# Spreading group B's scale factors with 64-column products whose stationary operand is one column at step zero

## The chip, the core and the metric

The kernel runs on one core of a Trainium2 chip. The metric is the device time of one execution in microseconds (us), smaller is better. Five engines work side by side: TensorE (PE) multiplies, VectorE (DVE) and ScalarE (ACT) work elementwise, GpSimd (POOL) does small work and SyncE (SP) starts the transfers. A matmul of PE takes a *stationary* operand (`lhsT`, loaded into the array) and a moving one (`rhs`, streamed through), and writes to PSUM.

## The reference, cut to what matters

Two layers, each with three groups of attention heads (A, B, C), an output projection and a feed-forward part. The change touches group B, differential attention:

```python
def diff_block(qb1, qb2):
    p = (softmax(scores(qb1, k1_all, sb)) - lam * softmax(scores(qb2, k2_all, sb)))
    return weigh(p, vb_all)

ob = sweep_blocks(diff_block, group(q1, B_HEADS), group(q2, B_HEADS))
ob = rmsnorm(ungroup(ob), g_subln) * (1.0 - lam_init)
```

There are 512 latent tokens and 256 context tokens, four B heads of 64 columns. In the second layer the context tokens need no output.

## The kernel before, in words

Group B goes two heads and 256 query tokens at a time (`attn_b`). There are ten such pieces: six in layer 0 (two pairs of heads, each with two pieces of latent and one of context queries) and four in layer 1. A piece makes scores `S` in PSUM, exponentials `P` on ACT, subtracts the second softmax from the first on DVE (`P1 = P2 * cf + P1`), transposes `P` on PE (products `T<-ident,P`), copies the transposes out (`pt`), and multiplies them with the values `V` into `acc`, a PSUM tile `T`. In `acc` the output lies transposed: partitions 0 to 63 are the first head, 64 to 127 the second, and the 256 columns are tokens.

Then comes the RMS norm of each token and head, a chain over all engines: ACT squares `acc` (`sqb`); PE sums the squares over each head's 64 partitions with two products whose moving operand `hsel` has two columns (written `T<-hsel,sqb`); DVE makes `ms` from these sums; POOL raises it to a power (`rs`, printed `t<-t,mhalf`). `rs` holds four factors per token: token on the partitions, (token block, head) in the columns. PE *spreads* them, that is brings them to the layout of `acc` (head's 64 partitions, token in the column), by a product with the identity. ACT or DVE copies the result out (`rsb`), and DVE multiplies `acc` with it into `o`, which the output projection reads after a split in high and low parts (`oh`, `ol`).

All instructions are recorded first and then put into one order by a planner (`Plan.schedule`), which prices every operation, looks which engine is free next and takes the ready operation that is earliest in the program's order, with an advance for score products. It also charges a fixed price where PE goes from products with 128 output partitions to products with 64 or 32, or back, and takes what is recorded under `plan.together()` as one piece. The engines then run their own queue in this order. All instructions therefore carry one line, L377, in the profile, and are told apart by tiles. Output tiles of 64 partitions were in the program before: the products with `V` are made in pairs, one head to partitions 0 to 63 and the other to 64 to 127. A stationary operand at step zero was there too: `T<-brow,ident` in the norm of A's queries and keys.

Of the kernel before, what the change touches and what calls it, by code (L numbers as in the profile page):

```python
# [47 lines left out]
MODE_AHEAD = 30  # L48
SA = 0.125
SB = 32.0 ** -0.5  # L50
SLOTS = {"u": 39, "pt": 8, "s": 7, "y": 24, "rb": 2, "S": 2, "T": 4, "ropeG": 1}


class _Op:
# [17 lines left out]
class Plan:  # L72
# [171 lines left out]
    def schedule(self):  # L244
# [8 lines left out]

        level = {tag: np.zeros(n + 1, np.int32) for tag in SLOTS}
        for t, a in self.first.items():
            level[self.tile_tag[t]][a:self.last[t] + 1] += 1
        for tag, lv in level.items():
            if lv.max() > SLOTS[tag]:
                raise ValueError(f"{tag}: {lv.max()} tiles alive of {SLOTS[tag]} at {ops[int(lv.argmax())].tag}")
        slots = {tag: [0.0] * b for tag, b in SLOTS.items()}  # L260
        t_end = dict.fromkeys(to_go, 0.0)
# [19 lines left out]
        while len(order) < n:  # L281
            best = None
            for e in sorted(free_at, key=free_at.get):
# [4 lines left out]
                while heap and len(seen) < 250:  # L288
# [21 lines left out]
                    for tag, ts in need.items():  # L310
# [5 lines left out]
                        at = max(at, sorted(slots[tag])[k - 1])  # L316
                        if b > frontier and level[tag][frontier:b].max() + k > SLOTS[tag]:
                            full[tag] = b
# [62 lines left out]
def dit_block(  # L381
# [8 lines left out]
    plan = Plan(nc, (  # L390
        x, c, ctx_in, c_ctx, w_ada, b_ada, g_attn, g_ffn, w_in, g_q, g_k, lam_q1, lam_k1, lam_q2, lam_k2,
        g_subln, sink_logit, w_out, w_ff1, w_ff3, w_ff2, g_final, k_ident, k_mask, k_ones, k_ropeA, k_ropeB, out))
    act, dve, pe, pool, sp = (plan.queue(e) for e in ("act", "dve", "pe", "pool", "sp"))
    act_dve, dve_pool = plan.queue("act|dve"), plan.queue("dve|pool")

    pools = {tag: ctx.enter_context(tc.tile_pool(name="p" + tag, bufs=SLOTS[tag])) for tag in ("u", "pt", "s", "y", "rb")}
    cp = ctx.enter_context(tc.tile_pool(name="cp", bufs=1))
    pools["S"] = ctx.enter_context(tc.tile_pool(name="pS", bufs=SLOTS["S"], space=PSUM))
    pools["T"] = ctx.enter_context(tc.tile_pool(name="pT", bufs=SLOTS["T"], space=PSUM))
# [4 lines left out]
    def nm(s):  # L404
        cnt[0] += 1
        return f"{s}{cnt[0]}_"

    def new(tag, shape, name, dt=F32):
        return plan.tile(pools[tag], [128] + list(shape), dt, tag, nm(name))

    def U(shape, dt=F32, name="u"):
        return new("u", shape, name, dt)
# [4 lines left out]
    def tiny(n):  # L417
        return new("y", [n], "t")
# [7 lines left out]
    def C(shape, name, dt=F32):  # L426
        return cp.tile([128] + list(shape), dt, tag=name, name=name)
# [13 lines left out]
    ident = C([128], "ident")  # L441
# [233 lines left out]
    for l in range(2):  # L675
# [71 lines left out]
        for ch, segs in enumerate(chunks):  # L747
            o = 0
# [67 lines left out]
        ropeG = plan.tile(cp, [128, 2, NX, 2, 64], F32, "ropeG", f"ropeG{l}")  # L816
# [197 lines left out]

        def spread(rps, o, rr, n):

            rb = new("rb", [6, 64], "rb")
            dve_pool.tensor_copy(rb[:, 0:2 * n], rr.rearrange("p (h o) -> p h o", o=1).to_broadcast([128, 2 * n, 64]))
            for j in range(n):
                pe.matmul(rps[:, o + 128 * j:o + 128 * j + 128],  # L1020
                          lhsT=rb[:, 2 * j:2 * j + 2].rearrange("p h d -> p (h d)"), rhs=ident, start=True, stop=True)

        def pv_pair(acc, Ps, off, heads, kbs):

# [85 lines left out]
        def attn_b():  # L1110
            for p, r, i0 in units(range(2)):
# [31 lines left out]
                rs = tiny(4)  # L1143
                pool.tensor_tensor(rs, ms, mhalf[:, 0:4], ALU.pow)
                spread(acc, 256, rs, 2)
                rsb = S2([256], "rsb")
                act_dve.copy(rsb, acc[:, 256:512])
# [113 lines left out]
        for r, i in ctx_first:  # L1261
# [14 lines left out]
            for j, kt in enumerate(range(KT)):  # L1276
                with plan.together():
                    for n, (st, wl) in enumerate(((oh, 0), (oh, 1), (ol, 0))):
                        for hf in range(2):
                            pe.matmul(ps[hf], lhsT=st[:, kt], rhs=wo[kt][wl][:, 512 * hf:512 * hf + 512],  # L1280
                                      start=(j == 0 and n == 0), stop=(j == KT - 1 and n == 2))
# [164 lines left out]
        for ft in range(FT):  # L1446
# [18 lines left out]
            for a in range(2):  # L1465
                if ft:
                    hs.append(PS())
                s = hs[a]
# [48 lines left out]
        for n, (r, i) in enumerate(qtiles):  # L1517
            plan.label = f"ffE{l}"
            xt = xt0[r, i]
            if last:  # L1520

                y, ss = U([1024], name="yo"), tiny(2)
# [82 lines left out]
```

## Time and profile before

| | us |
|---|---|
| median of 3 runs | 1688.7 (1687.33 to 1689.38) |
| the profiled execution's own time | 1688.15 |
| its span, first to last instruction | 1686.3 |
| PE busy | 1636.0 (97%) |
| DVE busy | 1308.3 (78%) |
| ACT busy | 724.6 (43%) |
| POOL busy | 117.9 (7%) |

The span leaves 1.85 us of the execution's own time around it. The busy shares are means over stages: projections and feed-forward part, where PE is all that counts, and two stretches of attention, about 200 to 390 us (layer 0) and 1140 to 1290 us (layer 1), where the four compute engines hand work to one another. Records of a PE product are longer than the distance to the next one, since products overlap: what a product costs is read from its start to the start of the next.

### The profile page before, as it was taken

The page shows a single profiled execution, that of the slowest core. Times are in us where ns is not written, and L with a number is a line of the kernel's source. Part 1 is how long each engine was busy: PE and PEld are TensorE (multiplying, and loading weights), DVE is VectorE, ACT ScalarE, POOL GpSimd, SP SyncE. Part 2 cuts the span into 40 slices and gives each one's busy share as a digit, 9 for nine tenths or more (in the row PEclk, how much of TensorE's full clock was granted, in tenths as well). Part 3 has the DMA queues.
Part 4 walks back from the last instruction along what each step waited for, and adds up shares of the span by engine and source line. Part 5 has one row for each costly group of instructions (what it writes and reads, how often), then busy time and mean ns, then how long its engine had stood idle before and what let it go on. Part 6 is the DMA issues. An engine that isn't in the chain of part 4 may idle for free.

```text
span 1686.3 us, 24082 instructions
## 1 busy us (share of the span) xinstructions
PE 1636.0 (97%) x9171; PEld 1330.1 (79%) x9171; DVE 1308.3 (78%) x2238; ACT 724.6 (43%) x1441; POOL 117.9 (7%) x167
## 2 busy tenths in 40 slices
PE   7999899999999999999999999999999999999998
PEld 4787667667898888888888888777777888888886
DVE  3776889776576997987768884788886668888896
ACT  3523888774354222323211152368884542232222
POOL 0130300100000000000000001121001000000010
PEclk9999999999999999999999999999999999999999
DMA  9512231225353554443323360112023534234261
GB/s 307 204 51 75 62 97 38 82 69 144 96 191 102 175 160 152 141 147 124 103 76 87 138 188 25 38 48 55 1 55 109 150 100 126 75 101 124 75 200 50
DMA packets 153278, 182.94 MB, mean 108 GB/s; under 512 B 9316, under 2 KB 121396, under 8 KB 153164
## 3 DMA queue, kind: packets, MB, share of 16 engines
q1 hardware_dynamic: 153164, 181.42, 34.8%
q8 instruction: 72, 1.18, 0.3%
q14 instruction: 42, 0.34, 0.1%
HBM read 163.00 MB, written 9.47 MB: 102 GB/s over the span
## 4 chain that ended last, share of the span: by engine, by line
PE 82%; DVE 4%; ACT 4%; issue 1%; DMA 0%; POOL 0%; DVEq 0%; SPq 0%; POOLq 0%; ACTq 0%
PE S__1355 L377 1%; PE S__1354 L377 1%; PE S__1543 L377 1%; PE S__1765 L377 1%; PE S__1841 L377 1%; PE S__1468 L377 1%; PE S__1691 L377 1%; PE S__1908 L377 1%; PE S__2047 L377 0%; PE S__2045 L377 0%; PE S__2036 L377 0%; PE S__2034 L377 0%; PE S__1969 L377 0%; PE S__1378 L377 0%; PE S__1365 L377 0%
## 5 line engine op out<-in xcount | busy, mean ns | idle before, releaser
L377 POOL TENSOR_TENSOR t__2091<-t__2090,mhalf 128x1 f32<-128x1 f32 x1 | 0.5, 548 | 513.8 <-DVE t__2090 L377 513.8
L377 POOL TENSOR_TENSOR ws__3615<-ws__3615,gate__3614 128x512 f32<-128x512 f32 x1 | 1.3, 1298 | 285.9 <-DMA ws__3618<-in_w_ff_dram 285.9
L377 DVE TENSOR_TENSOR wl__2247<-ws__2245,wh__2246 128x1024 fp32r<-128x1024 f32 x1 | 1.2, 1227 | 10.9 <-ACT V__2170 L377 10.9
L377 ACT ACT_TABLE_LOAD x6 | 7.7, 1283 | 0.8 <-PEq L1590 0.7
L377 DVE SCALAR_TENSOR_TENSOR acc__1463<-wa__1465,cstat,acc__1463 128x1024 f32<-128x1024 f32 x1 | 1.3, 1285 | 8.1 <-ACT acc__1463 L377 8.1
L377 DVE TENSOR_TENSOR t__2200<-qr__2199,ropeB 128x128 f32<-128x128 f32 x1 | 0.3, 292 | 9.2 <-ACT qr__2199 L377 9.2
L377 ACT ACTIVATE xn__2088<-xf__2066 128x1024 f32<-128x1024 f32 x1 | 1.1, 1060 | 13.5 <-issue 13.5
L377 ACT CAST fh__1972<-sg__1929 128x384 fp32r<-128x384 f32 x1 | 0.5, 514 | 12.7 <-DVE sg__1929 L377 12.7
L377 DVE TENSOR_TENSOR sg__1356<-sg__1356,S__1355 128x768 f32<-128x768 f32 x1 | 1.0, 954 | 5.8 <-ACT acc__1374 L377 5.8
L377 ACT ACTIVATE sg__1895<-S__1884 128x768 f32<-128x768 f32 x1 | 0.8, 812 | 10.9 <-PE S__1884 L377 10.9
L377 ACT ACTIVATE sg__1958<-S__1947 128x768 f32<-128x768 f32 x1 | 0.8, 812 | 10.8 <-PE S__1947 L377 10.8
L377 PE MATMUL T__115<-wa__116,cstat 128*32 128x128 f32 x8 | 0.7, 417 | 4.9 <-DVE t__98 L377 4.9
L377 ACT ACTIVATE sg__2021<-S__2010 128x768 f32<-128x768 f32 x1 | 0.8, 812 | 10.6 <-PE S__2010 L377 10.6
L377 ACT ACTIVATE sg__2035<-S__2034 128x768 f32<-128x768 f32 x1 | 0.8, 812 | 10.4 <-PE S__2034 L377 10.4
L377 ACT CAST gh__2002<-sg__1990 128x768 fp32r<-128x768 f32 x1 | 0.8, 837 | 9.6 <-DVE sg__1990 L377 9.6
L377 ACT CAST wh__1728<-ws__1727 128x1024 fp32r<-128x1024 f32 x1 | 1.1, 1052 | 8.6 <-DMA ws__1727<-in_w_ff_dram 8.6
L377 ACT CAST wh__1577<-ws__1576 128x1024 fp32r<-128x1024 f32 x1 | 1.1, 1052 | 8.5 <-PE T__1568 L377 8.5
L377 ACT CAST wh__1502<-ws__1501 128x1024 fp32r<-128x1024 f32 x1 | 1.0, 1047 | 8.3 <-PE T__1493 L377 8.3
L377 POOL TENSOR_TENSOR ropeG<-ropeA,gqk 128x64 f32<-128x64 f32 (+1 forms) x7 | 4.1, 608 | 7.0 <-DVE gqk L377 5.7
L377 ACT CAST wh__1656<-ws__1655 128x1024 fp32r<-128x1024 f32 x1 | 1.1, 1052 | 8.1 <-DVE yw__1408 L377 8.1
L377 ACT ACTIVATE acc__1687<-wa__1686,cstat 128x1024 f32<-128x1024 f32 x1 | 1.1, 1150 | 7.8 <-PE T__1667 L377 7.8
L377 ACT ACTIVATE acc__1837<-wa__1836,cstat 128x1024 f32<-128x1024 f32 x1 | 1.1, 1150 | 7.8 <-PE T__1813 L377 7.8
(14049 smaller groups left out, 6742.8 us busy)
## 6 DMA issues: line engine op xcount, KB each, us to landing
x__83<-in_x_dram SPq DMA_DIRECT2D x1, 512.0 KB
x__84<-in_x_dram SPq DMA_DIRECT2D x1, 512.0 KB
x__131<-in_x_dram SPq DMA_DIRECT2D x1, 512.0 KB
x__136<-in_x_dram SPq DMA_DIRECT2D x1, 512.0 KB, 6.4
x__198<-in_ctx_dram SPq DMA_DIRECT2D x1, 512.0 KB
x__203<-in_ctx_dram SPq DMA_DIRECT2D x1, 512.0 KB
ws__240<-in_w_in_dram SPq DMA_DIRECT2D x1, 512.0 KB
ws__243<-in_w_in_dram SPq DMA_DIRECT2D x1, 512.0 KB
```

The costliest lines, as they stand in the source:

```text
L377: getattr(self.real[op.eng], method)(*args, **kw)
```

## The change

`spread` no longer makes `rb`, the tile in which each factor is repeated 64 times along the columns (ten copies of 128x256, on DVE or POOL as the planner chose). The stationary operand is the column of `rs` itself, read 64 times at step zero. For this each product of 128 output partitions is cut into two of 64, one per head, and a piece's four products go together.

```diff
-SLOTS = {"u": 39, "pt": 8, "s": 7, "y": 24, "rb": 2, "S": 2, "T": 4, "ropeG": 1}
+SLOTS = {"u": 39, "pt": 8, "s": 7, "y": 24, "S": 2, "T": 4, "ropeG": 1}
...
         def spread(rps, o, rr, n):
 
-            rb = new("rb", [6, 64], "rb")
-            dve_pool.tensor_copy(rb[:, 0:2 * n], rr.rearrange("p (h o) -> p h o", o=1).to_broadcast([128, 2 * n, 64]))
-            for j in range(n):
-                pe.matmul(rps[:, o + 128 * j:o + 128 * j + 128],
-                          lhsT=rb[:, 2 * j:2 * j + 2].rearrange("p h d -> p (h d)"), rhs=ident, start=True, stop=True)
+            with plan.together():
+                for j in range(n):
+                    for h in range(2):
+                        pe.matmul(rps[64 * h:64 * h + 64, o + 128 * j:o + 128 * j + 128],
+                                  lhsT=rr[:, 2 * j + h:2 * j + h + 1].to_broadcast([128, 64]), rhs=ident, start=True, stop=True)
```

Since the planner sees one step less between `rs` and the product, and other prices, it also orders the attention stretches anew. PE's order is the same up to the attention of layer 0, between the two attention stretches and after the second. Tile numbers are lower in the changed kernel, by 3 at the first spread and by one more with each that follows. Three places matter to the prediction.

The first spread of layer 0, on PE, at about 200 us; first before, then changed:

```order
L377 MATMUL T__433<-hsel,sqb__446 128x2 x2
L377 MATMUL T__488<-ident,stq__485 128x128 x2
L377 MATMUL T__488<-ident,stk__486 128x128 x2
L377 MATMUL S__575<-bkc__348,bqc__347 128x256 x2
L377 MATMUL T__618<-ident,stbq__619 128x128 x2
L377 MATMUL T__618<-ident,stbk__620 128x128 x2
L377 MATMUL S__579<-bkc__348,bqc__347 128x256 x2
L377 MATMUL T__433<-ident,rb__450 128x128 x2
L377 MATMUL T__621<-ident,stbq__622 128x128 x2
```

```order
L377 MATMUL T__430<-hsel,sqb__443 128x2 x2
L377 MATMUL T__484<-ident,stq__481 128x128 x2
L377 MATMUL T__484<-ident,stk__482 128x128 x2
L377 MATMUL S__570<-bkc__345,bqc__344 128x256 x2
L377 MATMUL T__612<-ident,stbq__613 128x128 x2
L377 MATMUL T__612<-ident,stbk__614 128x128 x2
L377 MATMUL T__430<-ident,t__446 64x128 x4
L377 MATMUL S__574<-bkc__345,bqc__344 128x256 x2
L377 MATMUL T__615<-ident,stbq__616 128x128 x2
```

The spread (`T<-ident,rb`, now `T<-ident,t`) has moved ahead of one pair of score products.

The third of the four pieces of layer 1, on PE, at about 1223 us. Here `S<-kc`, `S<-kx` and `S<-maskR` are group C's scores, `T<-ident,P` transposes of C's exponentials. Before:

```order
L377 MATMUL S__2801<-maskR,identR 128x384
L377 MATMUL T__2730<-hsel,sqb__2743 128x2 x2
L377 MATMUL T__2772<-ident,P__2755 128x128
L377 MATMUL T__2772<-ident,P__2761 128x128
L377 MATMUL T__2772<-ident,P__2767 128x128
L377 MATMUL S__2806<-kc__2527,qx__2524 128x256 x2
...
L377 MATMUL S__2807<-maskR,identR 128x384
L377 MATMUL T__2730<-ident,rb__2747 128x128 x2
```

Changed:

```order
L377 MATMUL S__2783<-maskR,identR 128x384
L377 MATMUL T__2719<-hsel,sqb__2732 128x2 x2
L377 MATMUL T__2719<-ident,t__2735 64x128 x4
L377 MATMUL S__2788<-kc__2516,qx__2512 128x256 x2
L377 MATMUL S__2788<-kx__2514,qx__2512 128x384
```

Twenty rows of scores and transposes stood between the sums and the spread; now the spread stands directly behind the sums on which it depends.

The end of layer 1's attention, on PE, at about 1270 us: `T<-pt,V` are the products with the values of the last piece but one, `T<-ident,P` the transposes of the last piece, `T<-wh,oh`, `T<-wl,oh`, `T<-wh,ol` the output projection. Before:

```order
L377 MATMUL T__2914<-pt__2926,V__2170 64x256 x2
L377 MATMUL T__2959<-ident,P__2929 128x128
L377 MATMUL T__2959<-ident,P__2944 128x128
L377 MATMUL T__2959<-ident,P__2935 128x128
L377 MATMUL T__2959<-ident,P__2950 128x128
```

Changed:

```order
L377 MATMUL T__2902<-pt__2914,V__2161 64x256 x2
L377 MATMUL T__3001<-wh__2967,oh__2999 128x512
L377 MATMUL T__3002<-wh__2967,oh__2999 128x512
L377 MATMUL T__3001<-wl__2968,oh__2999 128x512
L377 MATMUL T__3002<-wl__2968,oh__2999 128x512
L377 MATMUL T__3001<-wh__2967,ol__3000 128x512
L377 MATMUL T__3002<-wh__2967,ol__3000 128x512
L377 MATMUL T__2947<-ident,P__2917 128x128
L377 MATMUL T__2947<-ident,P__2932 128x128
L377 MATMUL T__2947<-ident,P__2923 128x128
L377 MATMUL T__2947<-ident,P__2938 128x128
```

Six products of the output projection have come ahead of the transposes. On DVE, at the same place, before:

```order
L377 CAST wh__2980<-ws__2979 128x1024
L377 SCALAR_TENSOR_TENSOR t__2957<-t__2927,nlam,t__2956 128x2
L377 CAST wh__2983<-ws__2982 128x1024
L377 SCALAR_TENSOR_TENSOR P__2944<-P__2945,t__2957,P__2944 128x768
L377 SCALAR_TENSOR_TENSOR P__2950<-P__2951,t__2957,P__2950 128x768
L377 TENSOR_TENSOR wl__2981<-ws__2979,wh__2980 128x1024
```

Changed:

```order
L377 CAST wh__2967<-ws__2966 128x1024
L377 SCALAR_TENSOR_TENSOR t__2945<-t__2915,nlam,t__2944 128x2
L377 TENSOR_TENSOR wl__2968<-ws__2966,wh__2967 128x1024
L377 SCALAR_TENSOR_TENSOR P__2932<-P__2933,t__2945,P__2932 128x768
L377 SCALAR_TENSOR_TENSOR P__2938<-P__2939,t__2945,P__2938 128x768
```

One cast has gone from ahead of the two subtractions, and the difference `wl` has come ahead of them.

## Rows read from the trace of the kernel before

**Rows 1.** The page: span, and busy time and instructions of each engine.

```profile
span 1686.3 us, 24082 instructions
PE 1636.0 (97%) x9171; PEld 1330.1 (79%) x9171; DVE 1308.3 (78%) x2238; ACT 724.6 (43%) x1441; POOL 117.9 (7%) x167
```

**Rows 2.** Windows over both attention stretches: length, busy per engine, PEclk, DMA, GB/s.

```profile
200.00:390.00 190.00, 177.50 (x1305) 128.18 (x1306) 158.95 (x353) 149.88 (x383) 18.66 (x30) 0.98 0.31 84
...
1140.00:1290.00 150.00, 143.03 (x983) 106.72 (x980) 128.30 (x259) 120.66 (x270) 18.85 (x27) 0.98 0.20 50
```

**Rows 3.** Waits of PE, 195 to 390 us: releaser, total, times, longest.

```profile
PE S__546 L377 <- ACT P__578 L377: 2.9, 1, 2.9
PE S__1184 L377 <- ACT P__1168 L377: 1.9, 1, 1.9
...
PE S__579 L377 <- ACT P__513 L377: 1.4, 1, 1.4
```

**Rows 4.** Windows of 10 us at the end of layer 1's attention, columns as above.

```profile
1260.00:1270.00 10.00, 10.00 (x78) 7.02 (x76) 9.43 (x15) 8.25 (x18) 2.12 (x2) 1.00 1.03 252
1270.00:1280.00 10.00, 6.23 (x34) 5.01 (x32) 10.00 (x15) 6.22 (x13) 0.80 (x1) 0.66 0.69 161
```

**Rows 5.** Timeline of PE there: start, duration, operation, [idle before and releaser].

```profile
1274.27 0.48 PE L377 MATMUL T__2959<-ident,P__2944 128*128 128x128 f32 x1 [3.53 <-DVE P__2944 L377]
...
1278.88 0.42 PE L377 MATMUL T__2969<-ident,P__2929 128*128 128x128 f32 x1
1279.09 0.42 PE L377 MATMUL T__2969<-ident,P__2944 128*128 128x128 f32 x1
```

**Rows 6.** Timeline of DVE there.

```profile
1273.21 1.01 DVE L377 SCALAR_TENSOR_TENSOR P__2944<-P__2945,t__2957,P__2944 128x768 f32<-128x768 f32 x1
...
1275.07 1.21 DVE L377 TENSOR_TENSOR wl__2981<-ws__2979,wh__2980 128x1024 fp32r<-128x1024 f32 x1
```

**Rows 7.** The tile of the first spread: its copy, minimum/median/maximum in ns.

```profile
L377 DVE COPY rb__450<-t__449 x1: 295/295/295, 200.6 to 200.6; 128x256 f32<-128x256 f32 x1
```

**Rows 8.** Timeline of PE around a step-zero operand and a spread of layer 0.

```profile
239.61 0.63 PE L377 MATMUL T__456<-brow,ident 24*32 24x256 f32 x8
240.17 0.50 PE L377 MATMUL S__741<-kx__460,qx__458 128*128 128x512 f32 x1
...
241.32 0.60 PE L377 MATMUL T__594<-ident,rb__603 128*128 128x128 f32 x4
241.76 0.27 PE L377 MATMUL T__660<-ident,P__637 128*128 128x128 f32 x1
241.87 0.27 PE L377 MATMUL T__660<-ident,P__644 128*128 128x128 f32 x1
```

**Rows 9.** Timeline of PE: from a transpose to paired products of 64 output partitions.

```profile
243.30 0.27 PE L377 MATMUL T__676<-ident,P__671 128*128 128x128 f32 x1
243.51 0.65 PE L377 MATMUL T__651<-pt__653,V__214 128*64 128x256 f32 x4
...
246.34 0.60 PE L377 MATMUL T__651<-pt__659,V__215 128*64 128x256 f32 x4
246.77 0.60 PE L377 MATMUL T__651<-pt__661,V__216 128*64 128x256 f32 x4
```

**Rows 10.** Timeline of PE from two of layer 1's sums; one spread, one projection product.

```profile
1222.84 0.50 PE L377 MATMUL T__2730<-hsel,sqb__2743 128*128 128x2 f32 x4
1223.20 0.31 PE L377 MATMUL T__2772<-ident,P__2755 128*128 128x128 f32 x1
...
1226.08 0.61 PE L377 MATMUL T__2730<-ident,rb__2747 128*128 128x128 f32 x4
...
1283.70 0.39 PE L377 MATMUL T__3015<-wh__2980,ol__3013 128*128 128x512 f32 x1
1283.93 0.50 PE L377 MATMUL T__2958<-hsel,sqb__2971 128*128 128x2 f32 x4
```

**Rows 11.** Timeline of POOL: the power behind each of these two sums.

```profile
1224.01 1.01 POOL L377 TENSOR_TENSOR t__2746<-t__2745,mhalf 128x4 f32<-128x4 f32 x1 [6.52 <-DVE t__2745 L377]
...
1284.79 2.05 POOL L377 TENSOR_TENSOR t__2974<-t__2973,mhalf 128x4 f32<-128x4 f32 x1 [12.12 <-DVE t__2973 L377]
```

More of the change, by code (lines that the diff above doesn't have):

```diff
@@ L394, in dit_block @@
     act_dve, dve_pool = plan.queue("act|dve"), plan.queue("dve|pool")
-    pools = {tag: ctx.enter_context(tc.tile_pool(name="p" + tag, bufs=SLOTS[tag])) for tag in ("u", "pt", "s", "y", "rb")}
+    pools = {tag: ctx.enter_context(tc.tile_pool(name="p" + tag, bufs=SLOTS[tag])) for tag in ("u", "pt", "s", "y")}
     cp = ctx.enter_context(tc.tile_pool(name="cp", bufs=1))
```

## The prediction, made before the changed kernel had run

> **What bounds the kernel now.** The page comes first: PE is busy 97% of the span, so the time is PE's work plus what it waits [rows 1]. The view by windows shows where it waits: 177.5 of 190 us busy in layer 0's attention and 143.0 of 150 in layer 1's, so about 12.5 and 7 us of idle time lie there, while DVE is busy 84% and 86% and ACT 79% and 80% of these stretches [rows 2]. The change acts only there. The list of PE's waits then says which engine ends them: in layer 0 mostly ACT, by an exponential `P` that scores wait for (2.9, 1.9 and 1.4 us) [rows 3]. In layer 1 one wait stands out, 3.53 us at 1274 us for DVE's `P__2944` [rows 5]; the windows show that the granted clock falls there from 1.00 to a mean of 0.66 [rows 4]. No spread is on either list as a waiting instruction of any weight. Before, PE had enough other work between the sums of squares and the spread: at 1223 us from 1223.20 to 1226.08, 2.88 us, while POOL's power ended at 1225.02 [rows 10, 11].
>
> **The products themselves.** A spread costs 0.44 us of PE today (241.32 to 241.76, four records, two for each product) [rows 8]. Afterwards it is eight records of half the columns. Products of 64 output partitions already run in pairs side by side: four records of 256 columns take 0.43 us (246.34 to 246.77), half of what one after another would take [rows 9]. I price the new spread by this row: again 0.43 us, change nothing. If they ran one after another it would be 0.43 more each, 10 x 0.43 = +4.3; that end goes to a rival. The zero step costs nothing by the nearest row: eight records of 128 columns in 32-wide pieces with `brow` take 0.56 us to the next product [rows 8], which is 0.43 of work and a switch of 0.1 (next); the bound above is that 0.13 per spread, 1.3 in all, if it were the step.
>
> **Switches.** From one transpose to the next PE needs 0.11 us (241.76 to 241.87) [rows 8]; from the last transpose to products of 64 partitions 0.21 (243.30 to 243.51) [rows 9]. So a change of output width costs 0.10. Along PE's order there are 15 more of them than before (91 to 100 in layer 0's attention, 60 to 66 in layer 1's); that is fewer than two per spread because some spreads stand next to value products. 15 x 0.10 = **+1.5** (0 if they all fall into waits). The Trainium skill (TensorEngine Tiling (Array Packing), Key Properties) speaks against this change: a change of tiling mode drains the engine. By that the price would be a product's whole record less its spacing, 0.27 - 0.11 = 0.16, hence 15 x 0.16 = 2.4 and a sum 0.9 higher; the row has 0.10, and I follow the row.
>
> **The copies.** Ten `rb` copies go, eight on DVE at 0.28 to 0.35 us (0.295 at the first) [rows 7] and two on POOL. 8 x 0.29 = 2.3 us leave an engine that is 85% busy and that ends the largest wait of layer 1 [rows 2, 5]; what is saved ahead of such a wait is saved in full, elsewhere nothing. POOL is busy a tenth, so its two count for nothing. I take **-1.0** (0 to -2.3).
>
> **Where the spreads stand now.** The step between power and product has gone, and the planner puts products close behind the sums. What must be covered is sums to the power's end less the sums' own 0.36 (1222.84 to 1223.20): 1225.02 - 1222.84 - 0.36 = 1.82 at the third piece of layer 1, and 1286.84 - 1283.93 - 0.36 = 2.55 at its fourth, where the power takes 2.05 instead of 1.01 [rows 10, 11].
> At the first spread of layer 0 the product moves into the 1.4 us wait of the scores behind it [rows 3]: **-0.4** (its own 0.44 [rows 8]; 0 if its factors come only at the wait's end).
> At the other five of layer 0, PE's work in between, counted by the order and priced by such spacings, goes from 2.9 to 4.9 us to 2.0, 2.1, 2.3, 3.1 and 3.4. With 1.82 that hides, with 2.55 the first three lack 0.55 + 0.45 + 0.25. I take **+0.3** (0 to 1.25).
> In layer 1 the cover becomes 2.2, 1.6, 0 and 1.4 us (was 2.2 to 4.1). Third piece: nothing stands between, so PE waits 1.82 and the handing over, **+1.9**, against none today; behind it wait C's scores, then ACT's exponentials. Fourth: six projection products, 6 x 0.23 (1283.70 to 1283.93) = 1.4 [rows 10], against 2.55 or, with the short power, 1.5: 0.1 to 1.2, **+0.5**. Second: 0.25 to 1.0, **+0.6**. First: 0 to 0.35, **+0.2**.
>
> **Where orders moved otherwise.** At 364 us of layer 0 scores move ahead of value products and their wait of 1.9 us [rows 3] moves to the next scores; walking through ACT's order I find gain and loss alike, 0 (-1 to +1). At the end of layer 1's attention six projection products come into the place of the 3.53 us wait [rows 5], but DVE now makes the 1.21 us `wl` ahead of the two subtractions (and one cast less) [rows 6], so these come half a microsecond later. Going through both queues with the durations of these rows, PE's waits come to 2.75 instead of 3.53 + 0.24. That is -1.0. Transposes also ran 0.21 apart there instead of 0.11 (1278.88 to 1279.09) [rows 5, 8]: the lower of the clock's two levels, 1.2 GHz, for 23 of them, 2.4 us in all, after PE had idled 3.5 us. With the idle time broken up by products I give it half a chance not to fall, -1.2. Together **-2.2** (0 to -3.8).
>
> **Sum.** +1.5 - 0.4 + 0.3 + 1.9 + 0.5 + 0.6 + 0.2 - 2.2 - 1.0 = **+1.4 us**, so the span goes from 1686.3 to 1687.7, the profiled execution from 1688.15 to 1689.55, and the median, 0.55 above that execution, from 1688.7 to **1690.1**. A measurement of this kernel can tell about 0.2%, 3.4 us, from no change, so this is none (1685.3 to 1692.1).
>
> **Rivals.**
> *The chain behind the sums stays long everywhere* (slower, 0.30). One mechanism: POOL's power takes 2.05 us, as beside DVE's `wl` at 1284.79, and not 1.01 [rows 11], so every spread needs a cover of 2.55. Layer 1 then pays 2.55 + 1.15 + 1.0 + 0.35 = 5.05 and layer 0 1.25, 6.3 in place of 3.5: sum +4.2, **1692.9**. Without the tail's -2.2 it is 1695.1. It decides from +3.4 on, which is reached when the chain is some 0.3 us longer at each of the seven tight places. For it: the covers were cut to about the chain's best case. Against: the power at 1224.01 took 1.01, and a spread that waits gives its wait back where the next product would have waited anyway. The Trainium skill (GPSIMD Engine Reference, Key points) names a cause: POOL shares its SBUF interfaces with DVE, and contends with DVE's instructions of two SBUF inputs, which `wl` is; the trace agrees at 1284.79.
> *The tail heals* (faster, 0.18). If the clock never falls at 1270 us and the copies' 2.3 us all count, the terms are +1.5 - 0.4 + 0 + 1.9 + 0.1 + 0.25 + 0 - 3.8 - 2.3 = -2.75, and -3.75 with the better end at 364 us: **1685.0**. For it: DVE ends that wait, and six products fill it. Against: the subtractions come later than before.
> *The halves run one after another* (slower, 0.06): the change then doubles what it was to leave alone, +1.4 + 4.3 = +5.7, **1694.4**. Against it stand the pairs of value products [rows 9].
>
> **How the numbers follow.** No measurable change has 0.46. Slower: 0.30 + 0.06 = 0.36. Faster: 0.18. The likeliest case by itself spans 1686.5 to 1692. The range must reach into both others: down to 1683.5 (the healing tail and 1.5 us of shorter waits in layer 0), up to 1697.0 (the long chain without the tail's gain, 1695.1, and the upper bounds at 364 us, +1, and of the switches, +0.9); one in ten may lie outside on either side.
>
> **What would show it.** PE's timeline at the new spreads: eight records within 0.45 to 0.65 us say side by side, 0.9 says the opposite. PE's waits should list `T<-ident,t` for POOL's power: 1.8 to 2.0 us at the third piece of layer 1 (some 20 rows earlier than 1226), 0.3 to 1.2 at the second and fourth, next to nothing in layer 0. POOL's powers: 1.0 or 2.0. The window 1270 to 1280 shows whether the clock keeps 1.0, and the wait for DVE's `P` whether it fell below 1 us. DVE should be busy 2.3 us less over the two stretches. I am wrong if waits that I count singly cancel: a spread that waits 1.9 us lets ACT and DVE catch up, so that PE's later waits shrink; or if the new order makes a wait at a place where PE has none today, which the trace of before cannot show.

## The result, and the profile after

The changed kernel takes 1698.74 us, the median of 4 runs (1695.89 to 1701.69), against 1689.04 for the kernel before on the same chip (1687.33 to 1690.07): a ratio of 1.006, with a 95% interval of 1.0047 to 1.0073. It is slower by 9.7 us, where 1690.1 and a range up to 1697.0 had been forecast. The profiled execution is the fastest of the changed kernel's runs, 1695.89, 7.7 us above the one profiled before; it shows the lesser part of the loss.

Its page begins with the span and the busy times, which answer to [rows 1]:

```profile
span 1694.0 us, 24169 instructions
...
PE 1636.5 (97%) x9211; PEld 1325.2 (78%) x9211; DVE 1310.8 (77%) x2230; ACT 722.7 (43%) x1440; POOL 120.5 (7%) x166
```

PE is busy as long as before (1636.0 us), and the span is 7.7 us longer: the loss is idle time of PE. DVE is busy 2.5 us longer although eight copies have left it, since the new plan also gives the engines other work: of the 210 copies of transposes (`pt`) DVE now makes 79, before 69. "New order" below includes that. Between products that stand alike in both programs, the stretch of layer 0's attention (149.66 to 379.67 us before) has grown by 2.7 us and that of layer 1 (1119.70 to 1299.86) by 3.5; the rest is spread over the other stretches.

By windows (busy time of PE, PE's loads, DVE, ACT, POOL; then the granted clock), the first two answering to [rows 2], the fourth to [rows 4]:

```profile
200.00:390.00 190.00, 175.14 (x1321) 124.61 (x1320) 156.43 (x344) 150.52 (x387) 20.24 (x29) 0.99 0.30 83
1140.00:1290.00 150.00, 139.17 (x980) 102.13 (x979) 130.56 (x264) 116.57 (x269) 19.78 (x29) 1.00 0.20 50
1220.00:1230.00 10.00, 7.76 (x58) 5.77 (x55) 6.78 (x20) 6.67 (x17) 1.66 (x2) 1.00 0.00 0
1270.00:1280.00 10.00, 10.00 (x80) 6.76 (x78) 8.71 (x16) 8.45 (x20) 2.15 (x3) 1.00 0.79 195
```

PE idles 14.9 us in the first stretch (12.5 before) and 10.8 in the second (7.0). Against that the end of layer 1 has healed: 1270 to 1280 us is fully busy at clock 1.00, where it was 0.66.

PE's waits, in layer 0 and then in layer 1 (who waits, for whom, total, times, longest), answer to [rows 3, 5]:

```profile
PE S__541 L377 <- ACT P__573 L377: 4.2, 1, 4.2
PE S__1180 L377 <- ACT P__1164 L377: 2.0, 1, 2.0
...
PE T__2719 L377 <- POOL t__2735 L377: 2.2, 1, 2.2
PE T__2720 L377 <- DVE P__2711 L377: 2.0, 1, 2.0
...
PE T__3001 L377 <- DVE t__2945 L377: 0.8, 1, 0.8
```

The 4.2 was 2.9. The 2.2 is the third spread of layer 1, forecast at 1.9. Of the other nine spreads only the first of layer 0 makes PE wait more than 0.1 us (0.25). The 2.0 for DVE's `P__2711` is new and in no term of the sum. The 3.5 us wait at layer 1's end is gone; four shorter ones there come to 2.0 us.

The timeline of PE and POOL at that third spread (start, duration, operation, idle time before and releaser) answers to [rows 10, 11]:

```profile
1227.34 0.50 PE L377 MATMUL T__2719<-hsel,sqb__2732 128*128 128x2 f32 x4
1230.07 0.66 PE L377 MATMUL T__2719<-ident,t__2735 128*64 128x128 f32 x8 [2.23 <-POOL t__2735 L377]
1230.66 0.50 PE L377 MATMUL S__2788<-kc__2516,qx__2512 128*128 128x256 f32 x2
...
1228.53 1.48 POOL L377 TENSOR_TENSOR t__2735<-t__2734,mhalf 128x4 f32<-128x4 f32 x1 [1.47 <-DVE t__2734 L377]
```

The new spread takes 0.59 us to the next product: side by side it is 0.43, and two changes of output width are some 0.08 each. So it looks as forecast (the wait is a little longer because the power took 1.48 us, not 1.01); what surrounds it has to be explained.

### The profile page after: what moved, and what is told of

The parts are those of the page before. It is cut to its first block, busy times and chain, and to the rows that moved or that the text cites. A ratio compares the mean times of both kernels' runs of the same rounds, so it can differ in the third digit from the quotient of the medians.

```text
span 1694.0 us, 24169 instructions
## 1 busy us (share of the span) xinstructions
PE 1636.5 (97%) x9211; PEld 1325.2 (78%) x9211; DVE 1310.8 (77%) x2230; ACT 722.7 (43%) x1440; POOL 120.5 (7%) x166
## 4 chain that ended last, share of the span: by engine, by line
PE 80%; ACT 4%; DVE 4%; DMA 2%; issue 1%; SPq 0%; POOL 0%; DVEq 0%; POOLq 0%; ACTq 0%
DMA ws__2984<-in_w_out_dram 1%; PE S__1346 L377 1%; PE S__1345 L377 1%; PE S__1534 L377 1%; PE S__1756 L377 1%; PE S__1832 L377 1%; PE S__1459 L377 1%; PE S__1899 L377 1%; PE S__1682 L377 1%; PE S__2038 L377 0%; PE S__2036 L377 0%; PE S__2027 L377 0%; PE S__2025 L377 0%; PE S__1960 L377 0%; PE S__1369 L377 0%
## 5 line engine op out<-in xcount | busy, mean ns | idle before, releaser
L377 ACT ACTIVATE xn__2079<-xf__2057 128x1024 f32<-128x1024 f32 x1 | 1.1, 1060 | 13.6 <-issue 13.6
L377 ACT ACTIVATE sg__1949<-S__1938 128x768 f32<-128x768 f32 x1 | 0.8, 812 | 10.8 <-PE S__1938 L377 10.8
L377 ACT ACTIVATE sg__2012<-S__2001 128x768 f32<-128x768 f32 x1 | 0.8, 812 | 10.6 <-PE S__2001 L377 10.6
L377 ACT ACTIVATE sg__1886<-S__1875 128x768 f32<-128x768 f32 x1 | 0.8, 812 | 10.6 <-PE S__1875 L377 10.6
```

The source lines that it names most:

```text
L377: getattr(self.real[op.eng], method)(*args, **kw)
```

## The experiments

All are compared with runs of the kernel before on their chip. *Growth* is that of the two stretches named above, layer 0 / layer 1, in the one profile of each run. It varies by itself: layer 0 has the order of before in seven of the profiles with new products, and grows there by -0.5 to 2.6 us. So the medians decide, and growth says where. In most of them the planner is shown one thing and the engines are given another. A recorded operation may carry a list `_now` of what is issued in its place:

```diff
-                for e, method, args, kw in op.calls:
-                    getattr(self.real[op.eng], method)(*args, **kw)
+                for e, method, args, kw in [c2 for c in op.calls for c2 in c[3].pop("_now", [(op.eng,) + c[1:]])]:
+                    getattr(self.real[e], method)(*args, **kw)
```

**The changed kernel once more.** No edit.

> The changed kernel once more, to see which of its waits come back. In the first profile the time from a product that stands alike in both programs to the next such product grew by 1.8 us in layer 0's attention, 3.5 us in layer 1's, and 2.2 us in the stretches around, where PE's order is the same. Theory A (the new order of the attention stretches costs it): the two attention stretches grow again by 1.5 to 4 us each, with the same waits (scores behind ACT at 209 us, the spread behind POOL at 1230 us, a transpose behind DVE at 1216 us). Theory C (chance outside attention): those waits shrink or the 2.2 us around them vary by several us between the two profiles. Time 1694 to 1702 by both.

1699.81 us (1699.09 to 1703.68); 1.007 (1.0057 to 1.0082); growth 5.0 / 5.6. Over both sets of runs one and the same program takes 1695.9 to 1703.7, the kernel before 1686.7 to 1690.6. The windows of this profile show one reason:

```profile
1230.00:1240.00 10.00, 8.76 (x60) 8.06 (x62) 7.66 (x19) 5.94 (x15) 1.18 (x1) 0.83 0.01 2
```

Behind the third spread's wait the clock falls here (0.83, so 1.7 us of full speed are missing in this window); in the first profile it did not. In layer 0's attention 5.1 us of full speed are missing in this profile and 1.7 in the first.

**New products, old order.** The planner is shown the old form; at issue the copy is dropped and the old products are replaced.

```diff
+            new_products = [("pe", "matmul", (rps[64 * h:64 * h + 64, o + 128 * j:o + 128 * j + 128],),
+                             {"lhsT": rr[:, 2 * j + h:2 * j + h + 1].to_broadcast([128, 64]), "rhs": ident,
+                              "start": True, "stop": True}) for j in range(n) for h in range(2)]
+            dve_pool.tensor_copy(rb[:, 0:2 * n], rr.rearrange("p (h o) -> p h o", o=1).to_broadcast([128, 2 * n, 64]), _now=[])
             for j in range(n):
                 pe.matmul(rps[:, o + 128 * j:o + 128 * j + 128],
...
+                          lhsT=rb[:, 2 * j:2 * j + 2].rearrange("p h d -> p (h d)"), rhs=ident, start=True, stop=True,
+                          _now=new_products[2 * j:2 * j + 2])
```

> The new products (four of 64 output partitions, step-zero stationary operand, no copy) put where the old ones stood, every other instruction in the order of the kernel before. Theory A (the order costs it): the loss goes away, 1686.5 to 1690.5, since ten copies leave DVE and POOL (0 to -2.3 us) and 20 changes of output width come (+0 to 2 us). Theory B (the products cost it: changes of width, half-width weight loads, step zero): 1694 to 1700, as the changed kernel, with the new spreads taking 1 us each on PE's timeline.

1689.68 us (11 runs, 1687.79 to 1691.95); 1.0004 (0.9995 to 1.0013); growth 1.0 / -0.4. It waits where the kernel before does; this is its longest wait in layer 1, as in [rows 5]:

```profile
PE T__2959 L377 <- DVE P__2944 L377: 3.5, 1, 3.5
```

The step-zero products, the switches and the missing copies together cost nothing that the times show. The loss is in the new order.

**Old products, new order.** The new plan, with the copy, on DVE, and the old products issued in the place of the new ones.

```diff
+            old = [("dve", "tensor_copy", (rb[:, 0:2 * n], rr.rearrange("p (h o) -> p h o", o=1).to_broadcast([128, 2 * n, 64])), {})]
...
+                                  _now=old if (j, h) == (0, 0) else [])
```

> The other way round: the order of the changed kernel with the old products, the copy made on DVE directly ahead of each spread. Theory A (order): as slow as the changed kernel or 1 to 3 us slower, 1696 to 1703, since at the spreads with little cover the copy of 0.3 us comes on top. Theory B (products): back to 1687 to 1691.

1708.32 us (1704.67 to 1709.23); 1.0111 (1.0097 to 1.0125). In this order the removal of the copy with its place in DVE's queue is worth 7 to 9 us, more than I had priced anywhere; in the old order, nothing. In its profile PE waits 0.9 us for the copy at each of the first two spreads of layer 1, where the changed kernel does not wait. But these runs also have a mean granted clock of 0.989, the changed kernel's 0.993: some 6 us of full speed, so most of the 7 to 9 us may be the clock.

**One layer at a time.** The planner sees the old form in layer 0 only, or (`l == 1`) in layer 1 only; the products are new in both.

```diff
+            if l == 0:
+                rb = new("rb", [6, 64], "rb")
...
+                return
```

> The new products everywhere; layer 0's attention in the order of before, layer 1's in the order of the changed kernel. Theory A with the shares of the first profile: layer 1's order is worth +3.5 us and layer 0's +1.8, so 1691 to 1694. If layer 0's order or what it shifts behind it carries most of the loss, 1687 to 1690; theory B (products) 1695 to 1700.

> The mirror image of the last run: layer 0's attention in the order of the changed kernel, layer 1's in the order of before, new products everywhere. By the profiles so far layer 0's new order is worth 1.8 to 4.9 us by itself: 1691 to 1694.5. If the loss is all in layer 1 (as the run with the old order in layer 0 says, which kept 10.7 us of it): 1688.5 to 1690.5.

New order in layer 1 alone: 1700.11 us (1697.88 to 1702.54), 1.0067 (1.0055 to 1.008), growth 0.9 / 10.6. In layer 0 alone: 1692.07 (1691.43 to 1694.64), 1.0019 (1.001 to 1.0028), growth 4.8 / 0.6. So most of the loss is layer 1's. The two losses, 11 and 3 us, add up to more than the changed kernel's 10 to 12.

**Piece by piece.** The new form is shown for one piece alone: the first of layer 0, or the first, second or third of layer 1.

```diff
-                spread(acc, 256, rs, 2)
+                spread(acc, 256, rs, 2, old=not (l == 0 and (p, r, i0) == (0, 0, 0)))
```

In layer 1 `(p, i0)` is (0, 0), (0, 2) or (1, 0).

> New products everywhere; the planner sees the new form at the first piece of layer 0 alone, so that the order differs from before only between 200 and 255 us, where the spread moves ahead of one pair of scores. By the prediction's step (the product moves into a wait of 1.4 us): 0.4 us faster than the old order with new products, 1688.5 to 1689.5. By the profiles since (scores wait 4.2 in place of 2.9 us for ACT behind it, and the clock falls there): 1690 to 1693.

> New products everywhere, the planner sees the new form at the first piece of layer 1 alone: covers of 2.2, 1.8, 1.5 and 2.7 us in layer 1, PE's order close to that of the changed kernel in the rest. If the order around the spreads, not the spreads' own cover, makes the loss (the 2 us wait for a subtraction at 1216 us, late weights at the end): 1694 to 1702. If cover does: 1688 to 1692.

> New products everywhere, the planner sees the new form at the second piece of layer 1 alone: covers of 4.8, 1.8, 1.0 and 1.4 us, a fourth order of layer 1. If short cover at the third spread costs: about half of the changed kernel's loss, 1692 to 1696. If not: 1688 to 1691, or 1697 to 1701 where this order brings the waits at 1216 us and at the end.

> New products everywhere; the planner sees the new form at the third piece of layer 1 alone. Order as before up to 1215 us, then new: 1.8 us of work ahead of the third spread (none in the changed kernel), and an end of the attention as in the changed kernel, with projection products among the last transposes. If the third spread's wait and the 2 us wait just ahead of it make the loss of layer 1: 1689 to 1691.5. If the new end makes it (weights late, more alternations between projection and transposes): 1693 to 1699.

| the new form in | median (us) | ratio (95%) | growth |
|---|---|---|---|
| layer 0, first | 1691.25 (11 runs) | 1.0017 (1.0008 to 1.0026) | 1.4 / -0.8 |
| layer 1, first | 1699.41 | 1.0063 (1.005 to 1.0076) | 2.6 / 9.2 |
| layer 1, second | 1695.55 | 1.0039 (1.0026 to 1.0053) | 0.9 / 4.3 |
| layer 1, third | 1688.26 (11 runs) | 0.9996 (0.9988 to 1.0005) | 0.9 / -2.4 |

The first of layer 0, whose order differs at 200 to 255 us alone, costs 2.9 us (0.0017 x 1689), by the medians 2.2 more than the same products in the old order (1.0004, intervals overlapping), where my term was -0.4. The third of layer 1, planned alone, gets other products behind its sums and costs nothing. The first and the second, for which I had +0.2 and +0.6, cost most when planned alone: each sends all that follows in layer 1 into another order, with waits in other places. The longest with the second alone:

```profile
PE T__3013 L377 <- DVE wl__2980 L377: 2.5, 1, 2.5
PE S__2756 L377 <- ACT P__2754 L377: 2.0, 1, 2.0
PE T__2814 L377 <- DVE P__2809 L377: 1.5, 1, 1.5
```

PE's idle time tells layer 1's orders apart. Here are the windows of the kernel before, the changed kernel, the new order in layer 1 alone, its first piece alone and its third alone:

```profile
1120.00:1315.00 195.00, 187.75 (x1225) 142.90 (x1224) 160.99 (x327) 146.30 (x337) 25.39 (x40) 0.98 0.23 60
1120.00:1315.00 195.00, 183.79 (x1222) 137.29 (x1221) 163.08 (x324) 140.94 (x327) 27.84 (x43) 1.00 0.20 51
1120.00:1315.00 195.00, 181.43 (x1190) 135.00 (x1189) 158.74 (x316) 138.99 (x322) 26.77 (x41) 0.97 0.20 51
1120.00:1315.00 195.00, 180.63 (x1196) 133.89 (x1196) 159.29 (x316) 140.04 (x324) 25.82 (x41) 0.99 0.20 51
1120.00:1315.00 195.00, 189.24 (x1252) 141.80 (x1251) 162.16 (x330) 147.27 (x340) 22.01 (x35) 1.00 0.23 59
```

PE idles 7.3, 11.2, 13.6, 14.4 and 5.8 us of these 195. With layer 1's old order and the new products it idles 7.2 us, in three profiles alike; with the second piece alone 11.7.

The first of layer 0 shows how. PE's sums of squares, the scores behind them and the exponential that the next scores wait for, in the kernel before:

```profile
197.58 0.50 PE L377 MATMUL T__433<-hsel,sqb__446 128*128 128x2 f32 x4
...
200.60 0.50 PE L377 MATMUL S__579<-bkc__348,bqc__347 128*128 128x256 f32 x2 [1.35 <-ACT P__513 L377]
...
205.57 0.47 ACT L377 ACTIVATE P__578<-S__579,t__580 128x256 f32<-128x256 f32 x1
```

ACT and PE there, in the kernel with that piece alone (its `P__577` is the `P__578` of before, its `S__578` the `S__579`):

```profile
198.18 0.51 PE L377 MATMUL T__433<-hsel,sqb__446 128*128 128x2 f32 x4
...
207.40 0.47 ACT L377 ACTIVATE P__577<-S__578,t__579 128x256 f32<-128x256 f32 x1 [0.97 <-POOL stbk__634 L377]
...
200.11 0.66 PE L377 MATMUL T__433<-ident,t__449 128*64 128x128 f32 x8 [0.26 <-POOL t__449 L377]
201.20 0.51 PE L377 MATMUL S__578<-bkc__348,bqc__347 128*128 128x256 f32 x2 [0.44 <-ACT P__512 L377]
...
208.02 0.79 PE L377 MATMUL S__545<-kx__459,qx__456 128*128 128x512 f32 x1 [4.22 <-ACT P__577 L377]
```

The 1.4 us wait of the scores does shrink, to 0.44, and they start as long behind the sums as before: 3.02 us. But between the scores' first exponential and the second, `P__577`, ACT now has three casts `stb` (one before) and the wait for POOL. That one starts 9.22 us behind the sums instead of 7.99, and the next scores wait 4.22 us instead of 2.91. The windows behind it:

```profile
205.00:210.00 5.00, 1.98 (x8) 1.25 (x12) 3.49 (x6) 3.58 (x13) 1.92 (x3) 0.56 0.16 64
210.00:215.00 5.00, 5.00 (x36) 4.22 (x29) 3.65 (x8) 2.75 (x6) 0.00 (x0) 0.76 0.34 105
```

Means of 0.56 and 0.76 leave 5 x 0.44 + 5 x 0.24 = 3.4 us of full speed missing; the same windows of the kernel before have 0.77 and 0.89, 1.7 us. That does not make the difference over the whole layer, though: the kernel before has a second fall (0.83 in 360 to 370 us) that this one has not (1.00), so that both miss 3.4 us.

**Is it the third spread's wait?** Three tries. In the first, that spread reads the constant column `mhalf` instead of the factors (so the piece is not normalised) and waits for no power:

```diff
+                        col = (mhalf if third else rr)[:, 2 * j + h:2 * j + h + 1].to_broadcast([128, 64])
```

> The changed kernel, but the third spread of layer 1 takes a constant column as its stationary operand in place of the factors, so that it waits for nothing on POOL; the norm's factors of this one piece are left out of the output. Theory A (the waits of the new order add up, and the clock falls behind some of them): the wait of 2.2 us goes, 1697 to 1698, and if the clock falls less often behind it, 1694 to 1697. Rival (the chain over DVE and ACT bounds that stretch anyway, PE waits a little later instead): 1699 to 1700, as the changed kernel.

1699.68 us (1695.29 to 1699.82); 1.0054 (1.0041 to 1.0067); growth 2.2 / 5.8. PE's waits:

```profile
PE T__2957 L377 <- ACT pt__2956 L377: 2.7, 1, 2.7
PE T__2720 L377 <- DVE P__2711 L377: 1.9, 1, 1.9
PE S__2788 L377 <- ACT P__2786 L377: 0.9, 1, 0.9
```

The wait has fallen to 0.7 us, and the time is handed on: 0.9 at the scores behind it, 2.7 at layer 1's end, where the changed kernel waited 0.2 and 0.9 in its two profiles. In the second try, made on the kernel with layer 1's new order alone, that spread stands nine products later and PE's order is otherwise the same:

```diff
+                spread(acc, 256, rs, 2, old=not (l == 1 and (p, i0) != (1, 0)))
```

> As the run with the old order in layer 0 (1700.1), but the planner sees the old form at the third piece of layer 1: PE's order then differs from that run in one thing, the third spread stands nine products later, with 1.5 us of work ahead of it in place of none. If the wait at this spread and what comes behind it (the clock) make most of layer 1's loss: 1690 to 1695. If it only hands its time to later waits, as the run with the constant column suggests: 1698 to 1702.

1697.87 us (1697.05 to 1700.36); 1.0057 (1.0044 to 1.0069); growth 0.9 / 8.8. The wait is the same 2.2 us, for another engine:

```profile
PE T__2967 L377 <- ACT pt__2966 L377: 2.7, 1, 2.7
PE S__2798 L377 <- ACT P__2796 L377: 2.2, 1, 2.2
PE T__2729 L377 <- DVE P__2720 L377: 2.0, 1, 2.0
```

So the wait at the spread as such adds 1.7 us by the medians (1.0067 to 1.0057), and, as the intervals overlap, perhaps nothing. In the third try the power is priced 1 us higher in the plan, so that the planner keeps other products between, with the new products and, to compare, with the old:

```diff
-            return n * 0.165 + 0.1
+            return n * 0.165 + 0.1 + 1.0
```

> The changed kernel's products, but the planner prices POOL's power 1 us higher, so that it puts 1.3 to 4.4 us of PE's work between sums and spread (third spread of layer 1: 1.5 in place of 0), in a third order. If cover behind the sums is what the change lost: 1687 to 1691. If the cost is that of leaving the order of before at all (waits elsewhere on DVE and ACT that any other order brings): 1693 to 1702.

> The kernel before, its copies and its products, but the planner prices POOL's power 1 us higher, so that covers are 1.5 to 5.5 us and both attention stretches are ordered anew. If the loss belongs to the spreads being close behind the sums: 1687 to 1691. If any new order of these stretches loses against the one of before, whatever the spreads are: 1693 to 1700.

New products: 1695.52 us (1692.76 to 1698.48), 1.0036 (1.0024 to 1.0047). Old products: 1694.69 (1694.05 to 1696.9), 1.0041 (1.0027 to 1.0054). With covers in place the new products still lose, and the old ones lose as much when merely planned anew: the order before is a good one, and two others of the same work cost 6 and 7 us.

**Does the clock count?** Eight useless products of `ident` with `ident`, into a free part of the bank, go where PE would wait: first in the third spread's wait of the changed kernel, then, in the kernel with layer 1's new order alone, in both waits at 1216 and 1230 us.

```diff
+                            now = [("pe", "matmul", (rps[:, 384:512],), dict(lhsT=ident, rhs=ident, start=True, stop=True))
+                                   for _ in range(8)] + now
```

> The changed kernel with eight products of no use (identity by identity, 1.8 us of PE's work, overwritten afterwards) in the wait of the same spread. The wait on POOL stays as long, but PE is busy in it. If falls of the clock behind this wait are part of the loss: the profile shows clock 1.00 behind it, and the time is 1 to 3 us below the changed kernel, 1696.5 to 1698.5. If only the waiting time itself counts: no change, 1699 to 1700.5.

> As the run with the old order in layer 0 (1700.1, clock low three times in its profile of layer 1), with eight products of no use in each of the two waits of 2 us at 1216 and 1230 us, so that PE is busy in them while they last as long. If the falls of the clock behind these waits are a large part of layer 1's loss: clock 1.00 there and 1694 to 1698. If only the waits count: 1699 to 1702.

One wait filled: 1696.98 us (1696.26 to 1698.59), 1.0047 (1.0035 to 1.006), growth 2.4 / 4.7; its interval overlaps those of the changed kernel. Two filled: 1695.66 (1691.85 to 1695.85), 1.0035 (1.0022 to 1.0048), against 1.0067 unfilled: 5.4 us less (0.0032 x 1689). Growth of layer 1 is 4.7 for 10.6, but in the profile of the fastest of its runs, 3.8 us below the median. Windows unfilled:

```profile
1210.00:1220.00 10.00, 7.77 (x45) 6.84 (x45) 7.36 (x14) 4.06 (x10) 1.93 (x2) 0.83 0.00 0
...
1230.00:1240.00 10.00, 10.00 (x63) 8.29 (x64) 7.63 (x18) 5.63 (x15) 0.00 (x0) 0.87 0.01 2
...
1290.00:1300.00 10.00, 7.51 (x39) 4.57 (x37) 5.84 (x6) 4.01 (x5) 0.00 (x0) 0.88 0.33 79
```

and filled:

```profile
1210.00:1220.00 10.00, 9.56 (x73) 7.68 (x73) 7.81 (x17) 4.52 (x11) 0.24 (x1) 1.00 0.00 0
...
1230.00:1240.00 10.00, 10.00 (x70) 7.05 (x68) 8.79 (x25) 6.76 (x16) 0.00 (x0) 1.00 0.00 1
...
1290.00:1300.00 10.00, 10.00 (x55) 7.37 (x54) 4.53 (x10) 2.70 (x5) 1.87 (x2) 1.00 0.00 0
```

The filling shortens no wait by itself, since the factors come no sooner. Where PE was kept at work, the clock stayed at 1.00 instead of 0.83 and 0.87. In this profile the fall in 1290 to 1300 us, which was not filled, is missing too; the wait ahead of it is 0.9 us instead of 2.5. Over all runs the mean granted clock is 0.994 filled and 0.992 unfilled, some 3 us of full speed; the rest of the 5.4 is not accounted for.

What one fall costs can be read from layer 0 in the profiles with new products and layer 0's old order. With one fall of 3.4 us at half clock it grew by -0.5 us (this profile), with two by 0.9 to 1.0 (five profiles), with three by 2.6 (the first piece of layer 1 alone). So one fall is worth some 1.5 us.

**The same in the kernel before.** Fourteen such products in the 3.53 us wait of [rows 5].

```diff
+                                pe.transpose(*targs, _now=fill * (14 * (tail and (n, h, i) == (0, 0, 1))) + [("pe", "transpose", targs, {})])
```

> The kernel before, with fourteen products of no use (3.1 us of PE's work) in its own longest wait, the 3.5 us at 1274 us of layer 1, written where the awaited transposes write afterwards. If the clock falls because PE idles there: it stays at 1.00, the 23 transposes behind it run 0.11 us apart in place of 0.21, and 2.4 us are saved: 1685.5 to 1687. If the clock falls for another reason: 1688 to 1690.

1687.15 us (11 runs, 1686.06 to 1689.2); 0.999 (0.9981 to 0.9999). The window and the transposes, which answer to [rows 4, 5]:

```profile
1270.00:1280.00 10.00, 9.11 (x80) 7.37 (x78) 10.00 (x15) 7.74 (x15) 0.80 (x1) 1.00 0.80 184
...
1277.17 0.27 PE L377 MATMUL T__2969<-ident,P__2929 128*128 128x128 f32 x1
1277.28 0.27 PE L377 MATMUL T__2969<-ident,P__2944 128*128 128x128 f32 x1
```

Clock 1.00 for 0.66, transposes 0.11 apart for 0.21: the term of 2.4 us that I had worked out from [rows 5] for this fall is about what is gained here (1.7 us, with an interval of 0.2 to 3.2). This is the fastest of the kernels run, by little.

**Late weights at layer 1's end.** The wait for `pt__2956`, 0.2 to 2.7 us in the profiles, lies behind ACT's casts of the out-projection's weights. ACT in the changed kernel:

```profile
1291.79 1.05 ACT L377 CAST wh__2985<-ws__2984 128x1024 fp32r<-128x1024 f32 x1 [1.19 <-DMA ws__2984<-in_w_out_dram]
1292.74 0.58 ACT L377 COPY pt__2956<-T__2955 128x512 f32<-128x512 f32 x1
```

The first of these loads is issued at 1255.31 before and 1271.43 now, 44.6 and 36.0 us ahead of the same product at the end of the attention. So I replaced them by constants written by POOL (layer 1's output projection then has no true weights):

```diff
+                now = [dict(_now=[("pool", "memset", (st, 0.01), {})]), dict(_now=[])] if last else [{}, {}]
```

> The changed kernel, but in layer 1 the weights of the output projection are set to a constant by POOL at the place where they would be loaded, so no transfer is waited for; the loads are left out. If late weights at the end of layer 1's attention (casts on ACT that wait for a transfer, with the copies of transposes queued behind them) are part of the loss: PE's waits for those copies, 0.2 to 2.7 us in the profiles so far, go, and the time is 1 to 3 us below the changed kernel, 1696.5 to 1699. If they are not: 1699 to 1701.

1702.21 us (1699.8 to 1704.36); 1.0079 (1.0065 to 1.0093). The wait for `pt__2956` is gone, but the substitute brought one of 4.7 us (last section), so the price of the late loads stays open.

## Why the prediction was wrong

**Right: the edit itself.** Products side by side (0.43 and two switches in 0.59), switches +1.5 against copies -1.0: the old order with the new products gives 1.0004, its interval -0.8 to +2.2 us, which holds the +0.5 of these terms. How it divides between them is not shown. One sign failed: DVE was to be busy 2.3 us less and is busy 2.5 more, because the new plan hands it other copies. The Trainium skill (TensorEngine Tiling (Array Packing), Key Properties) has a change of tiling mode drain the engine; the row shows a cost, 0.08 for each change, half of what I had worked out by that rule. The rival of the halves one after another is out.

**Right in place, wrong in sum: the third spread.** +1.9 was forecast, 2.2 came. But removed it comes back further on, and moved away it is a wait for ACT of the same length. The sum added it in full; the runs leave it 1.7 us by the medians, and perhaps nothing. The working had named this as a way to be wrong (waits that cancel).

**Wrong: the other spreads.** The waits that the sum gave to the five later spreads of layer 0 (+0.3) and to the first, second and fourth of layer 1 (+0.2, +0.6, +0.5) did not come: PE waits there less than 0.1 us, in both profiles of the changed kernel.

**Right: the tail of layer 1.** -2.2 was forecast for shorter waits and the clock. The waits there fell from 3.77 to 2.0 us, and the clock stays at 1.00 (3.4 us were missing at 1270 us). With the third piece alone planned anew the stretch shrinks by 2.4. A gain I had held half likely came, and the kernel still lost.

**Wrong: the first spread of layer 0.** "-0.4 ... its own 0.44" became +2.9 alone, or +2.2 above the old order. I looked at the wait that the product moved into, not at ACT's queue, which the plan had changed there too: casts and a wait for POOL stand ahead of the scores' second exponential, and the next scores wait 1.3 us more. The rest is not traced.

**Wrong: "Where orders moved otherwise".** This step failed most. It walked through two places, 364 us and the tail, and let the rest of the new order count for nothing; in layer 1 alone that order costs 11 us with products that cost nothing in the old one. There the new order makes the 2.0 us wait for `P__2711`, where DVE now reduces C's scores between one subtraction and the next:

```profile
1214.60 0.81 DVE L377 TENSOR_REDUCE t__2742<-S__2740 128x1 f32<-128x640 f32 x1
1215.33 1.01 DVE L377 SCALAR_TENSOR_TENSOR P__2711<-P__2712,t__2718,P__2711 128x768 f32<-128x768 f32 x1
```

(the timeline of DVE after; PE's transpose of it starts at 1216.40), and it issues the last weights later. That a new order could make a wait where PE had none, unseen in the trace of before, the working had said; it gave it no term. The first and second pieces, +0.2 and +0.6 in the sum, were priced as two short waits at their spreads; planned alone, they shift the order of the whole stretch and grow it by 9 and 4 us.

**Wrong: the clock as a gain only.** I counted the fall that would go, none that could come. The order of layer 1 has waits of about 2 us, and behind the same wait the clock falls in one execution and not in another: no window of the first profile from 1210 us on, one of the second, three of the kernel with layer 1 alone. That is 0 to 5 us in layer 1, and a good part of the 8 us between runs of one program: the run of 1695.89 had a mean granted clock of 0.995, that of 1703.68 one of 0.992, which is 5 us. Filling two waits took 5.4 us back. But over its nine runs the changed kernel's mean clock is 0.993, like that of the kernel before over fifteen: falls that went and falls that came cancel. So the gain of 1.2 did not come on the average, and the loss of 10 to 12 us is not the clock's.

**The rivals.** "The chain stays long everywhere" had the right sign, 1692.9, by another mechanism: it rested on powers of 2.05 us, and all but three took 1.01 (the three 1.40 to 1.72). The covers were short, but PE waited for two of the ten spreads only, and a long cover does not cure it (1.0036). The tail healed, as the second rival had it, and that did not make the kernel faster.

**What the time is made of.** PE's idle time from 1120 to 1315 us goes from 7.25 to 11.21 us, 4.0 more, in the windows of the two kernels; the fall that went gives back at most 3.4. Of the 3.5 seen, 2 to 3 are then left. Six more changes of output width are some 0.6 of it (the products are otherwise the same: 9211 against 9171, four more for each spread); the remainder was not tested by itself. Open too: how much of layer 1's loss are the late weights, and how the rest divides between its first two pieces, since the parts do not add up (11 and 3 us against 10 to 12).

## What to carry to other kernels

Where a planner orders the work, an edit of one operation is two changes, the operation and a new order; run the new operation in the old order first, for here it cost nothing and the new order 10 us. A wait that is removed or made is not its length in time: follow who is pushed back and who waits next, along each engine's queue, for the whole stretch and not at two places. A wait of 2 us on PE can also cost the clock behind it; a few useless products in such waits bought 1.7 us (0.2 to 3.2) in one kernel here and 5.4 in another.

## What the hardware showed unexpectedly

Beside POOL's memsets a cast of DVE took 4.69 us that takes 0.69 in the changed kernel (timelines of the kernel without the loads):

```profile
1283.19 4.69 DVE L377 CAST wh__2967<-ws__2966 128x1024 fp32r<-128x1024 f32 x1
...
1283.70 0.95 POOL L377 MEMSET ws__2978<- 128x1024 f32 x1
```

Six memsets ran from 1281.92 on, the last from 1286.39 for 0.95; the cast ended at 1287.88, half a microsecond behind it. The Trainium skill (SBUF — State Buffer, Who interferes with whom) says that DVE's casts can take the port pair that DVE shares with GpSimd, and that the second to issue then blocks until the first is done. The trace agrees that the cast was blocked, and goes further: four of the memsets started after the cast's start (from 1283.70 on) and still came first.

The falls of the clock differ between executions of one program: 1.00 and 0.83 at 1230 to 1240 us behind the same 2.2 us wait.
